# Five seven-product steps instead of four in each column pair of w_down's first half

## The chip, the cores and the metric

The kernel runs on one core of a Trainium2 chip. Its time is the device time of one execution, in microseconds. The engines are called as the profile calls them: PE is TensorE (matmuls; PEld is its weight load), DVE is VectorE, ACT is ScalarE, POOL is GpSimd, SP is the engine whose queue issues most DMAs.

## The reference

One decoder layer on 256 tokens of width 2048, in fp32: a mixing part with two groups of attention heads, and a channel mixer. Only the end of the channel mixer is touched here:

```python
h = rmsnorm(x, pre_ffn_g[l])
u = causal_dwconv(h @ w_up[l], conv_w[l], conv_b[l])
gate, val = jnp.split(u, 2, axis=-1)
y = (jax.nn.gelu(gate, approximate=True) * val) @ w_down[l]
x = x + rmsnorm(y, post_ffn_g[l])
```

`w_up` is 2048 x 11264, `w_down` is 5632 x 2048. Call the product of gelu(gate) and val G: 256 tokens x 5632.

## The kernel before

**Parts.** Every fp32 operand of a matmul is split into a high part (rounded to the matmul's type, a cast on ACT) and a low part (the rest, a subtraction on DVE; `split`, L286 to L288, and `w_split`, L107 to L124). A product is three matmuls: high by high, high by low, low by high (`products`, L973).

**Weights.** `w_load` (L70) fetches 512 KB, 128 x 1024 values, by a DMA on SP's queue into one of five `raw` buffers. `w_parts` (L79) gives one of five pairs of buffers `whi` and `wlo`. ACT casts `whi`, DVE subtracts into `wlo`, PE uses both.

**Stages.** The channel mixer runs in two halves of 22 blocks of 128 columns of G. For each half, first the up projection: eleven steps g of 256 columns, each with a gate and a val projection (`proj_T`), the convolution (`conv`), gelu and the product, after which two blocks of G are split into `G[2g]` and `G[2g+1]` (L950 to L952). A block holds G transposed: 128 channels on the partitions, 256 tokens high and 256 low in the free dimension. Then w_down, in two column pairs, n = 0 and n = 2: columns n and n + 1, 512 wide each, are made together. The first half leaves its sum in `y_sb`, the second half adds to it.

**Fours and sevens.** `four` (L1016) loads two row blocks of w_down for one column group and multiplies them by two token blocks: four products, 12 matmuls. For two column groups that is eight products, 24 matmuls. `seven` (L987) does the same two rows by two column groups by two token blocks in the seven products of Winograd's form, 21 matmuls. It wants sums on both sides. On G's side, with a11, a21 the two token blocks of block 2u and a12, a22 those of block 2u + 1: s1 = a21 + a22, s2 = s1 - a11, s3 = a11 - a21, s4 = a12 - s2. POOL makes them in the up stage (L946 to L949) for the first `most` steps g, and ACT and DVE split them into `sums`. On the weights' side DVE makes four differences in place in the two raw buffers (L998 to L1001), one after another; the blocks are split before (w11; w21 and w22) and after (t1 and t3; t4 and t2). The seven products use a11, a12, a22, s1, s2, s3 and s4; a21 itself is in none of them.

**Order in w_down.** `SEVENS[half][n // 2]` says at which steps i of a column pair a seven stands. A step is: the seven's first three products (a, b, e), a four for column n and a four for n + 1, then the seven's other four products (d, f, c, g). The sevens take the first rows u, the fours the rest, so with four sevens there are seven steps, with five there are six. After the last seven `fold` (L1023) adds the four shared banks into `y_sb`; after the last step `down` (L963, with L965) adds the banks b, g, e and h.

**Who orders what.** PE runs in the order of the program. The instructions of ACT, DVE, POOL and SP are ordered by a planner that goes by its own costs, and each engine then runs its list in that order, waiting for what is not ready.

Of the kernel before, what the change touches and what calls it, by code (L numbers as in the profile page):

```python
# [9 lines left out]
F32R = mybir.dt.float32r  # L10
BF16 = mybir.dt.bfloat16
AF = mybir.ActivationFunctionType
ALU = mybir.AluOpType
# [4 lines left out]
P = 128  # L18
# [6 lines left out]
NEG = -1e30  # L25
FHALF = 22
HOLD = 6
SEVENS = (((0, 1, 3, 4), (0, 1, 3, 4)), ((0, 1, 3, 4), (0, 2)))
LOW = (14, 4, 4, 4)
ROOM = 112  # L30

# [2 lines left out]
def hybrid_layer(ctx: ExitStack, tc: tile.TileContext, x, pre_mix_g, w_in, b_forget, sinks,  # L34
# [3 lines left out]
    pe, act, dve, pool, sp = nc.tensor, nc.scalar, nc.vector, nc.gpsimd, nc.sync  # L38
# [5 lines left out]
    main = ctx.enter_context(tc.tile_pool(name="main", bufs=1))  # L44
# [7 lines left out]
    def bank(tag="acc"):  # L52
        return ps.tile([P, 512], F32, tag=tag, bufs=4, name="bank_" + tag)
# [16 lines left out]
    def w_load(src, a, c, pin=False):  # L70
        raw = wp.tile([P, UNIT], F32, tag="raw", bufs=5, name="raw")
        i = sp.dma_start(raw[:, :a * c].rearrange("p (a c) -> p a c", a=a), src)
        if pin:
            tc.keep_in_program_order(i)
        return raw, a, c
# [53 lines left out]
    def w_rows(w, k0, a, c0, c):  # L129
        return w[k0 * P:(k0 + a) * P, c0:c0 + c].rearrange("(a p) c -> p a c", p=P)  # L130
# [155 lines left out]
    def split(hi, lo, src):  # L286
        act.copy(hi, src)  # L287
        dve.tensor_tensor(lo, src, hi.bitcast(F32), op=ALU.subtract)  # L288
# [531 lines left out]
    with tc.tile_pool(name="ffn", bufs=1) as fp:  # L820
# [46 lines left out]
        def first_gate():  # L867

            banks = [bank(), bank()]

            def v(x, t):
                return x.rearrange("p (h t c) -> p h t c", h=2, t=2)[:, :, t, :]

            def each(kts):
                for kt in kts:
                    for m, b in enumerate(banks):
                        yield kt, b, slice(m * P, (m + 1) * P)

            def gate_high(t, *kts):
                for kt, b, ms in each(range(*kts)):  # L880
                    pe.matmul(v(b, t), gate[kt][0][:, ms], v(hT[:, kt, 0:512], t),  # L881
                              start=(t == 0 and kt == 0), stop=False)

            def gate_low(u):
                for kt, b, ms in each(range(u * 4, u * 4 + 4)):
                    pe.matmul(b[:, 256:512], gate[kt][1][:, ms], hT[:, kt, 0:256],
                              start=False, stop=(kt == KT - 1))

            gate_high(0, KT)
            for high, low in [turn(1, u) for u in range(4)]:  # L890
                high()
                low()
            lows[2]()
            x_squares(1)
            rows = ffn_tables()
            gate_high(1, 1)
            gate_low(0)
            gate_low(1)
            gate_high(1, 1, 4)
            gate_low(2)  # L900
            gate_high(1, 4, KT)
            gate_low(3)
            later(3, rows)
            return banks
# [3 lines left out]
        for half in range(2):  # L908
            G = [fp.tile([P, 512], F32R, tag="G", bufs=FHALF, name=f"G{j}")[:, 0:512]
                 for j in range(FHALF)]  # L910
            most = max(len(at) for at in SEVENS[half])
            if half:
                sums = main.tile([P, 4, 1024], F32R, tag="x", name="sums")
            for g in range(FHALF // 2):
                c0 = (half * (FHALF // 2) + g) * 256
                alt = (g + half) % 2
                if half == 0 and g == 0:
                    bg = first_gate()
                    order.__exit__(None, None, None)
                    bv = [bank(), bank()]  # L920
                    proj_T(w_up, DFF + c0, bv, LONG)
                else:
                    bg = [bank("att"), bank("att")] if alt else [bank(), bank()]
                    proj_T(w_up, c0, bg, LONG)
                gates = []
                for m in range(2):
                    y = conv(bg[m], c0 // P + m, "yg")
                    act.activation(y, y, AF.Gelu_apprx_tanh)
                    gates.append(y)
                if half or g:  # L930
                    bv = [bank("att"), bank("att")] if alt else [bank(), bank()]
                    proj_T(w_up, DFF + c0, bv, LONG)
                ys = []
                for m in range(2):
                    y = conv(bv[m], 44 + c0 // P + m, "yv")
                    dve.tensor_tensor(y, y, gates[m], op=ALU.mult)
                    ys.append(y)
                if g < most:
                    if half == 0 and g == 0:
                        for t in range(2):  # L940
                            sp.dma_start(x_dram[t * P:(t + 1) * P, :], x_sb[:, t, :])
                        sums = main.tile([P, 4, 1024], F32R, tag="x", name="sums")
                    s = fp.tile([P, 512], F32, tag="s", name="s")
                    (a11, a21), (a12, a22) = [(y[:, 0:P], y[:, P:256]) for y in ys]
                    s1, s2, s3, s4 = (s[:, i * P:i * P + P] for i in range(4))
                    pool.tensor_tensor(s1, a21, a22, op=ALU.add)  # L946
                    pool.tensor_tensor(s2, s1, a11, op=ALU.subtract)
                    pool.tensor_tensor(s3, a11, a21, op=ALU.subtract)
                    pool.tensor_tensor(s4, a12, s2, op=ALU.subtract)  # L949
                for m, y in enumerate(ys):  # L950
                    gt = G[g * 2 + m]
                    split(gt[:, 0:256], gt[:, 256:512], y)  # L952
                if g < most:
                    split(sums[:, g, 0:512], sums[:, g, 512:1024], s)
            if half == 1:
                rest = main.tile([P, KT, 512], F32R, tag="hT", name="rest")
                gbf = fp.tile([P, D], F32, tag="gbc", name="gbc_ffn")
# [21 lines left out]
            def parts_of(k, t):  # L979
                return G[k][:, t * P:(t + 1) * P], G[k][:, 256 + t * P:256 + (t + 1) * P]  # L980

            def split_into(dst, src, n):
                hi, lo = (x[:, :n * 512] for x in dst)
                split(hi, lo, src[:, :n * 512])
                return [(hi[:, i:i + 512], lo[:, i:i + 512]) for i in range(0, n * 512, 512)]

            def seven(n, u, last, banks, opened):  # L987

                b, e, g, a, c, d, f = banks
                k = half * FHALF + u * 2  # L990
                top, low = [w_load(w_rows(w_down, k + i, 1, n * 512, 1024), 1, 1024)[0]
                            for i in range(2)]
                b11, b12, b21, b22 = (x[:, i:i + 512] for x in (top, low) for i in (0, 512))
                s1, s2, s3, s4 = [(sums[:, u, i * P:i * P + P],
                                   sums[:, u, 512 + i * P:640 + i * P]) for i in range(4)]
                (w11,) = split_into(w_parts(UNIT, held=False), top, 1)
                w21, w22 = split_into(w_parts(UNIT, held=False), low, 2)
                dve.tensor_tensor(b11, b12, b11, op=ALU.subtract)  # L998
                dve.tensor_tensor(b12, b22, b12, op=ALU.subtract)
                dve.tensor_tensor(b22, b22, b11, op=ALU.subtract)  # L1000
                dve.tensor_tensor(b21, b21, b22, op=ALU.subtract)  # L1001
                products(a, parts_of(u * 2, 0), *w11, opened, last)
                products(b, parts_of(u * 2 + 1, 0), *w21, opened)
                products(e, s4, *w22, opened)

                def others():
                    t1, t3 = split_into(w_parts(UNIT, held=False), top, 2)
                    t4, t2 = split_into(w_parts(UNIT, held=False), low, 2)
                    products(d, s1, *t1, opened, last)
                    products(f, s3, *t3, opened, last)  # L1010
                    products(c, s2, *t2, opened, last)
                    products(g, parts_of(u * 2 + 1, 1), *t4, opened)

                return others
# [30 lines left out]
            for n in (0, 2):  # L1045
                opened = []
                tail = half and n
                at = SEVENS[half][n // 2]
                shared = [bank("att") for _ in range(4 if at else 0)]
                b, e, g = [bank() for _ in range(3)]  # L1050
                h = None if tail else bank()
                for i in range(FHALF // 2 - len(at)):
                    others = None
                    if i in at:
                        u = at.index(i)
# [68 lines left out]
        for t in range(2):  # L1124
            i = sp.dma_start(x_sb[:, t, :], x_dram[t * P:(t + 1) * P, :])
# [5 lines left out]
        v = before_last(0, 3)  # L1131
# [5 lines left out]
        for h in range(2):  # L1137
            if h:
                v = before_last(1, 4)
# [38 lines left out]
```

## Time and profile before

| | us |
|---|---|
| median of 3 runs | 1058.31 (1058.13 to 1058.46) |
| profiled execution | 1058.56 |
| its span, first to last instruction | 1056.8 |
| PE busy | 1046.5 |
| DVE busy | 820.8 |
| ACT busy | 635.5 |
| POOL busy | 259.0 |
| first half's up projections and its w_down, in the span | about 345 to 576 and 576 to 690 |

The profile is one execution, taken by the hardware profiler. Its span leaves out what lies before the first and after the last instruction. Rows of a timeline give start and duration in us, the engine, the line of the kernel, the operation and the tiles it writes and reads; in brackets stands the idle time before it and what ended it. A row of a group gives the count, the busy time and the mean duration in ns. Matmuls overlap: one of 512 columns is shown with 0.39 us, and its neighbour starts sooner than it ends.

### The profile page before, as it was taken

The numbers are of one execution on the slowest core, as the hardware profiler recorded it, in microseconds if no ns is written. First come the engines' busy times: TensorE is split into PE (matmuls) and PEld (weight loads), VectorE is DVE, ScalarE is ACT, GpSimd is POOL, SyncE is SP. The second block draws the span as 40 slices with busy tenths as digits, with TensorE's granted clock in tenths as the row PEclk, the third lists the DMA queues.
The fourth block names the chain that finished last, engine by engine and source line by source line (L and its number), as shares of the span: only waits on it lengthen the run. The fifth ranks groups of instructions, "written<-read, shape, count | busy, mean of one in ns | idle before, by whom it ended". The sixth has DMA issues, their size and how long they took to land.

```text
span 1056.8 us, 16351 instructions
## 1 busy us (share of the span) xinstructions
PE 1046.5 (99%) x5920; PEld 910.4 (86%) x5920; DVE 820.8 (78%) x1324; ACT 635.5 (60%) x1094; POOL 259.0 (25%) x282
## 2 busy tenths in 40 slices
PE   9999999999999999999999999999999999999996
PEld 7889988888889888888888888888888888888786
DVE  5989877886468787777768888867787777788983
ACT  7777757767557656656555555546566565655560
POOL 4253245431122433311112000003432221200301
PEclk9999999999999999999999999999999999999999
DMA  8645666655875766666665566766656665647483
GB/s 291 194 124 180 181 191 202 175 153 161 298 237 186 220 202 196 201 186 199 193 199 149 188 221 204 235 198 192 187 179 210 192 198 186 192 149 233 156 274 126
DMA packets 161965, 207.09 MB, mean 196 GB/s; under 512 B 6844, under 2 KB 131036, under 8 KB 160860
## 3 DMA queue, kind: packets, MB, share of 16 engines
q1 hardware_dynamic: 161564, 205.65, 62.0%
q8 instruction: 46, 0.75, 0.3%
q10 hardware_dynamic: 320, 0.40, 0.1%
q14 instruction: 35, 0.29, 0.1%
HBM read 201.68 MB, written 4.21 MB: 195 GB/s over the span
## 4 chain that ended last, share of the span: by engine, by line
PE 89%; DVE 4%; DMA 2%; issue 2%; ACT 1%; POOL 0%; SPq 0%; DVEq 0%; POOLq 0%; ACTq 0%
PE bank_acc L262 21%; PE bank_att L262 15%; PE bank_acc L284 13%; PE bank_acc L975 12%; PE bank_acc L269 11%; PE bank_att L269 7%; PE bank_att L975 2%; DMA raw<-in_w_down_dram 2%; DVE wlo L121 1%; PE bank_att L450 1%; PE bank_att L485 1%; PE bank_att L494 1%; DVE wlo L288 1%; PE bank_acc L881 1%; PE bank_acc L225 1%
## 5 line engine op out<-in xcount | busy, mean ns | idle before, releaser
L121 DVE TENSOR_TENSOR wlo<-raw,whi 128x1024 fp32r<-128x1024 f32 (+3 forms) x329 | 400.6, 1231 | 121.5 <-ACT whi L118 114.3
L118 ACT CAST whi<-raw 128x1024 fp32r<-128x1024 f32 (+3 forms) x328 | 333.5, 1033 | 174.6 <-issue 84.5
L262 PE MATMUL bank_acc<-hT,whi 128*128 128x512 f32 x1024 | 245.5, 392 | 0.0
L262 PEld LDWEIGHTS bank_acc<-hT,whi 128*128 128x128 f32 x1024 | 188.2, 188 | 37.1
L857 POOL TENSOR_TENSOR u<-u,rowf 128x256 f32<-128x256 f32 x88 | 95.6, 1107 | 440.1 <-DVE u L856 437.2
L262 PE MATMUL bank_att<-hT,whi 128*128 128x512 f32 x704 | 165.7, 390 | 0.0
L975 PE MATMUL bank_acc<-whi,G 128*128 128x512 f32 x492 | 159.5, 389 | 0.0
L262 PEld LDWEIGHTS bank_att<-hT,whi 128*128 128x128 f32 x704 | 130.6, 188 | 26.2
L269 PEld LDWEIGHTS bank_acc<-hT,wlo 128*128 128x128 f32 x1024 | 123.5, 188 | 3.2
L269 PE MATMUL bank_acc<-hT,wlo 128*128 128x256 f32 x1024 | 125.8, 278 | 0.0
L975 PEld LDWEIGHTS bank_acc<-whi,G 128*128 128x128 f32 x492 | 92.4, 188 | 19.0
L975 PE MATMUL bank_acc<-wlo,G 128*128 128x512 f32 x246 | 95.9, 390 | 0.4 <-DVE wlo L121 0.4
L269 PEld LDWEIGHTS bank_att<-hT,wlo 128*128 128x128 f32 x704 | 83.6, 188 | 1.9
L269 PE MATMUL bank_att<-hT,wlo 128*128 128x256 f32 x704 | 84.0, 277 | 0.0
L284 PE MATMUL bank_acc<-whi,oT 128*128 128x512 f32 (+1 forms) x272 | 81.8, 379 | 0.0
L287 ACT CAST whi<-raw 128x1024 fp32r<-128x1024 f32 (+1 forms) x56 | 51.7, 942 | 35.2 <-PE bank_acc L975 15.9
L288 DVE TENSOR_TENSOR wlo<-raw,whi 128x1024 fp32r<-128x1024 f32 (+1 forms) x56 | 62.2, 1133 | 6.5 <-ACT whi L287 6.5
L284 PEld LDWEIGHTS bank_acc<-whi,oT 128*128 128x128 f32 x272 | 50.2, 188 | 9.3
L975 PEld LDWEIGHTS bank_acc<-wlo,G 128*128 128x128 f32 x246 | 46.2, 188 | 10.2 <-DVE wlo L121 0.8
L284 PE MATMUL bank_acc<-wlo,oT 128*128 128x512 f32 (+1 forms) x136 | 51.2, 377 | 0.0
L859 ACT ACTIVATE yg<-u,cw 128x256 f32<-128x256 f32 x44 | 26.5, 602 | 37.2 <-POOL u L857 37.2
L284 PE MATMUL bank_acc<-whi,hT 128*128 128x384 f32 (+1 forms) x192 | 46.9, 323 | 0.0
(250 smaller groups left out, 1317.7 us busy)
## 6 DMA issues: line engine op xcount, KB each, us to landing
raw<-in_w_up_dram SPq DMA_DIRECT2D x176, 512.0 KB, 4.5
raw<-in_w_down_dram SPq DMA_DIRECT2D x88, 512.0 KB, 4.9
raw<-in_w_in_dram SPq DMA_DIRECT2D x51, 512.0 KB, 5.0
raw<-in_w_out_dram SPq DMA_DIRECT2D x32, 512.0 KB, 4.6
raw<-in_w_in_dram SPq DMA_DIRECT2D x16, 384.0 KB, 3.3
cb<-c_dram SPq DMA_DIRECT2D x8, 256.0 KB, 4.5
x_sb<-in_x_dram SPq DMA_DIRECT2D x2, 1024.0 KB, 6.0
x_dram<-x_sb SPq DMA_DIRECT2D x2, 1024.0 KB, 5.8
```

What stands on the lines that cost most here:

```text
L118: i1 = act.copy(hi[:, cs], raw[:, cs])
L121: i2 = dve.tensor_tensor(lo[:, cs], raw[:, cs], hi[:, cs].bitcast(F32), op=ALU.subtract)
L225: pe.matmul(b, hi[:, a, m * P:(m + 1) * P], hT[:, kt, 0:512], start=(kt == 0), stop=(kt == KT - 1))
L262: pe.matmul(b, hi[:, a, m * P:(m + 1) * P], hT[:, kt, 0:512], start=(kt == 0), stop=(last == (0, kt)))
L269: pe.matmul(b[:, 256:512], lo[:, a, m * P:(m + 1) * P], hT[:, u * 4 + a, 0:256], start=False, stop=(last == (1, u * 4 + a)))
L284: pe.matmul(b, a, r[:, cols], start=(first and i == 0), stop=(last and i == 2))
L287: act.copy(hi, src)
L288: dve.tensor_tensor(lo, src, hi.bitcast(F32), op=ALU.subtract)
L450: pe.matmul(sb[e][:, cs], a[r, t * P:(t + 1) * P], b[r, 0:nk], start=(n == 0), stop=(n == 2))
L857: pool.tensor_tensor(u[:, 2:258], u[:, 2:258], rowf, op=ALU.mult)
L859: act.activation(y, u[:, 2:258], AF.Identity, bias=cw[:, 3, ch:ch + 1], scale=cw[:, 2, ch:ch + 1])
L975: pe.matmul(b, x, r, start=b not in opened and not i, stop=closes and i == 2)
```

## The change

In the first half, each column pair gets five sevens, at steps 0 to 4, instead of four at steps 0, 1, 3 and 4. So the fifth pair of row blocks moves from fours to a seven, and a column pair has six steps instead of seven. The second half keeps its sevens.

Five sums of 4 KB a partition would not fit into the 16 KB of `sums`. In the first half s1 is therefore written over a21 in the product's own tile, before G is split, and takes a21's place in the block of G; `sums` keeps s2, s3 and s4, 384 wide, high and low 3 KB. In both halves POOL's instruction for s3 comes first, since it reads a21, and s1 stands last in `s` and `sums`.

```diff
-SEVENS = (((0, 1, 3, 4), (0, 1, 3, 4)), ((0, 1, 3, 4), (0, 2)))
+SEVENS = (((0, 1, 2, 3, 4), (0, 1, 2, 3, 4)), ((0, 1, 3, 4), (0, 2)))
...
-                sums = main.tile([P, 4, 1024], F32R, tag="x", name="sums")
+                sums = main.tile([P, 4096], F32R, tag="x", name="sums")
...
                     (a11, a21), (a12, a22) = [(y[:, 0:P], y[:, P:256]) for y in ys]
-                    s1, s2, s3, s4 = (s[:, i * P:i * P + P] for i in range(4))
+                    s2, s3, s4, s1 = (s[:, i * P:i * P + P] for i in range(4))
+                    if not half:
+                        s1 = a21
+                    pool.tensor_tensor(s3, a11, a21, op=ALU.subtract)
                     pool.tensor_tensor(s1, a21, a22, op=ALU.add)
                     pool.tensor_tensor(s2, s1, a11, op=ALU.subtract)
-                    pool.tensor_tensor(s3, a11, a21, op=ALU.subtract)
                     pool.tensor_tensor(s4, a12, s2, op=ALU.subtract)
                 for m, y in enumerate(ys):
                     gt = G[g * 2 + m]
                     split(gt[:, 0:256], gt[:, 256:512], y)
                 if g < most:
-                    split(sums[:, g, 0:512], sums[:, g, 512:1024], s)
+                    w = 384 + 128 * half
+                    split(*(sums[:, i * w:i * w + w] for i in (2 * g, 2 * g + 1)), s[:, :w])
...
-                s1, s2, s3, s4 = [(sums[:, u, i * P:i * P + P],
-                                   sums[:, u, 512 + i * P:640 + i * P]) for i in range(4)]
+                w = 384 + 128 * half
+                s2, s3, s4, s1 = [[sums[:, v * w + i * P:v * w + i * P + P]
+                                   for v in (2 * u, 2 * u + 1)] for i in range(4)]
+                if not half:
+                    s1 = parts_of(u * 2, 1)
```

More of the change, by code (lines that the diff above doesn't have):

```diff
@@ L941, in hybrid_layer @@
                             sp.dma_start(x_dram[t * P:(t + 1) * P, :], x_sb[:, t, :])
-                        sums = main.tile([P, 4, 1024], F32R, tag="x", name="sums")
+                        sums = main.tile([P, 4096], F32R, tag="x", name="sums")
                     s = fp.tile([P, 512], F32, tag="s", name="s")
                     (a11, a21), (a12, a22) = [(y[:, 0:P], y[:, P:256]) for y in ys]
-                    s1, s2, s3, s4 = (s[:, i * P:i * P + P] for i in range(4))
+                    s2, s3, s4, s1 = (s[:, i * P:i * P + P] for i in range(4))
+                    if not half:
+                        s1 = a21
+                    pool.tensor_tensor(s3, a11, a21, op=ALU.subtract)
                     pool.tensor_tensor(s1, a21, a22, op=ALU.add)
                     pool.tensor_tensor(s2, s1, a11, op=ALU.subtract)
-                    pool.tensor_tensor(s3, a11, a21, op=ALU.subtract)
                     pool.tensor_tensor(s4, a12, s2, op=ALU.subtract)
```

## The prediction

> **What bounds the kernel now.** I read the page's busy times first, then what TensorE (PE) waited for over the whole span.
>
> ```profile
> PE 1046.5 (99%) x5920; PEld 910.4 (86%) x5920; DVE 820.8 (78%) x1324; ACT 635.5 (60%) x1094; POOL 259.0 (25%) x282
> PE bank_acc L173 <- DVE junk L168: 1.3, 1, 1.3
> PE bank_att L494 <- DVE pl L288: 0.5, 1, 0.5
> PE bank_acc L975 <- DVE wlo L121: 0.4, 1, 0.4
> ```
>
> PE is busy for 99% of the span, and its named waits come to 2.2 us. So a matmul less is time less, as long as the others keep PE fed. The stretches view of the first half's w_down stage (columns: us of the stretch; busy us and count of PE, PEld, DVE, ACT, POOL; clock; DMA share; GB/s) and the chain of waits at the end of its first column pair (start, us, what) say the same of the place that changes:
>
> ```profile
> 575.50:692.00 116.50, 116.50 (x516) 96.47 (x515) 100.37 (x116) 63.17 (x69) 2.22 (x2) 1.00 0.65 210
> ```
> ```profile
> 612.67 6.80 PE bank_acc L975 x30
> 619.48 2.04 PE bank_att L975 x9
> 621.51 11.56 PE bank_acc L975 x51
> 633.08 0.68 PE bank_att L975 x3
> ```
>
> PE has no gap here, its clock is 1.00, and a 512-column matmul takes 6.80/30 = 0.2267 us. DVE is busy for 100.37 of 116.50 us: it is the engine with the least room. ACT and the DMAs have much more.
>
> **Matmuls removed.** Two fours (rows u of columns n and n+1) are 24 matmuls; a seven in their place is 21. One more seven in each of two column pairs saves 6 x 0.2267 = **1.36 us**. The matmul count should fall from 5920 to 5914. The 44 loads of 512 KB in this stage stay 44: a seven's two rows replace one load of each four.
>
> **DVE and ACT work added.** Groups of this stage (count | busy us, mean ns | idle before):
>
> ```profile
> L121 DVE TENSOR_TENSOR wlo<-raw,whi 128x1024 fp32r<-128x1024 f32 x32 | 38.9, 1222 | 11.5 <-ACT whi L118 11.2
> L288 DVE TENSOR_TENSOR wlo<-raw,whi 128x1024 fp32r<-128x1024 f32 x23 | 27.6, 1222 | 3.6 <-ACT whi L287 3.6
> L998 DVE TENSOR_TENSOR raw<-raw 128x512 f32<-128x512 f32 x7 | 4.8, 690 | 0.2
> L288 DVE TENSOR_TENSOR wlo<-raw,whi 128x512 fp32r<-128x512 f32 x7 | 4.8, 685 | 1.3 <-ACT whi L287 1.3
> L118 ACT CAST whi<-raw 128x1024 fp32r<-128x1024 f32 x31 | 32.6, 1054 | 30.9 <-PE bank_acc L975 21.6 <-DMA raw<-in_w_down_dram 5.5 <-PE bank_att L975 2.1
> L287 ACT CAST whi<-raw 128x512 fp32r<-128x512 f32 x7 | 4.3, 620 | 2.6 <-DMA raw<-in_w_down_dram 2.5
> ```
>
> A seven costs DVE three 1024-wide low parts, one 512-wide and four differences: 3 x 1.22 + 0.69 + 4 x 0.69 = 7.1 us. The two fours cost 2.45. So DVE gets 4.6 us more in each pair, and ACT (3 x 1.05 + 0.62) - 2 x 1.05 = 1.7 us more. ACT's hides in the 30.9 us that it waits before L118, mostly for PE to free a weight buffer. DVE's is the question: in a loop step with a seven it does 7.1 + 2.45 = 9.5 us of work under 45 matmuls, 10.2 us. Neighbours on DVE overlap by some 0.08 us (two L121 end 2.35 us after the first starts, below, not 2.44), which makes it about 9.1, so DVE gains some 1 us on PE in a step, if it never idles. Five such steps now follow one another, where the third was a pause of fours with 2.3 us of DVE work under 5.4 us of matmuls.
>
> By the Trainium skill, "VectorE: DVE Perf Modes", section "The perf-mode tier table", an fp32 tensor_tensor from SBUF runs at 1x, 2293 ns for 2048 elements. By that figure the step's 7,680 elements are an estimated 8.6 us, a margin of 1.6 us instead of 1; the rows say 9.1 to 9.5, and I use the rows.
>
> **Where that shows first: the third step of pair one.** DVE's and PE's timelines (start, us, line, out<-in [idle before <- releaser]):
>
> ```profile
> 591.27 1.05 ACT L287 CAST whi<-raw 128x1024 fp32r<-128x1024 f32 x1 [2.42 <-DVE raw L1001]
> 592.35 1.23 DVE L288 TENSOR_TENSOR wlo<-raw,whi 128x1024 fp32r<-128x1024 f32 x1 [1.19 <-ACT whi L287]
> 604.38 2.96 DVE L288 TENSOR_TENSOR wlo<-raw,whi 128x1024 fp32r<-128x1024 f32 x3
> 611.30 2.35 DVE L121 TENSOR_TENSOR wlo<-raw,whi 128x1024 fp32r<-128x1024 f32 x2
> ```
> ```profile
> 595.06 0.39 PE L975 MATMUL bank_att<-wlo,sums 128*128 128x512 f32 x1
> 598.46 0.39 PE L975 MATMUL bank_acc<-wlo,G 128*128 128x512 f32 x1
> ```
>
> The last unit of the second seven is ready on DVE at 593.58 and its low part is used at 595.06, a lead of only 1.5 us. Today DVE then has two fours to do. With a seven there, PE reaches the first four's low part after 3 + 6 + 2 matmuls more, at 598.46. DVE needs for w11, four differences, w21/w22 and that four what it took at the fifth step: from 606.74 (the second of the three at 604.38 ends, 0.60 before the third) to 612.52 (the first of the two at 611.30 ends), 5.78 us. 593.58 + 5.78 = 599.36: **0.9 us late**. If the planner puts the four ahead of the last two differences, as it did in some steps, it is 1.4 us sooner and nothing is late. Bounds 0 and 0.9; I take 0.3, nearer to none, because in the other steps of this pair DVE got each four done in time.
>
> The loads are next in question: SP issues one when DVE is through with a buffer, and a seven keeps its two until its last low parts. SP's waits, the loads of this stage (median us to landing) and ACT's longest wait for one:
>
> ```profile
> SPq L72 <- DVE wlo L121: 78.9, 36, 6.1
> raw<-in_w_down_dram SPq DMA_DIRECT2D x38, 512.0 KB, 4.9
> 599.70 1.05 ACT L118 CAST whi<-raw 128x1024 fp32r<-128x1024 f32 x1 [2.80 <-DMA raw<-in_w_down_dram]
> ```
>
> Buffers come free in the same order as now, so the load that lands before 599.70 becomes the top row of the fourth step's seven, wanted by PE only at 606.6. Cost nothing; were it a four of the third step, up to the 2.8 us.
>
> **And the border to pair two.** After the last seven there are now two fours, 24 matmuls or 5.44 us, less until pair two, while the four reads of the fold (L1029 to L1032) and the four of L965 stay (group first, then the timelines):
>
> ```profile
> L965 DVE TENSOR_TENSOR y_sb<-bank_acc,y_sb 128x512 f32<-128x512 f32 x8 | 5.1, 682 | 0.0
> ```
> ```profile
> 613.57 2.35 DVE L288 TENSOR_TENSOR wlo<-raw,whi 128x1024 fp32r<-128x1024 f32 x2
> 617.88 1.23 DVE L121 TENSOR_TENSOR wlo<-raw,whi 128x1024 fp32r<-128x1024 f32 x1 [0.82 <-ACT whi L118]
> 620.70 1.23 DVE L121 TENSOR_TENSOR wlo<-raw,whi 128x1024 fp32r<-128x1024 f32 x1 [1.59 <-ACT whi L118]
> 622.67 1.23 DVE L121 TENSOR_TENSOR wlo<-raw,whi 128x1024 fp32r<-128x1024 f32 x1 [0.15 <-ACT whi L118]
> 633.47 1.28 DVE L965 TENSOR_TENSOR y_sb<-bank_acc,y_sb 128x512 f32<-128x512 f32 x2
> ```
> ```profile
> 620.90 0.39 PE L975 MATMUL bank_att<-wlo,sums 128*128 128x512 f32 x1
> 634.27 0.39 PE L975 MATMUL bank_acc<-whi,sums 128*128 128x512 f32 x1
> ```
>
> From 615.92 to the third read of L965 (633.47 + 0.68 = 634.15) are 18.2 us, 2.56 of them idle; without two L121 (2.3) the work is 13.4 us. PE used the unit of 615.92 at 620.90 and needs that bank at 634.27; 5.44 us sooner, that is 615.92 + 12.9. So the bank e is freed **0.5 us late**, if the order stays; with that read ahead of the L121 before it, not at all. Bounds 0 and 0.8 (0.8 if the lead at the last seven is 0.3 us shorter); I take 0.2. Pair two's end has no such border: there up-projection units follow, whose DVE work is light. Sum of the stalls: **0.5 us, bounds 0 and 1.7**.
>
> **The up stage.** A fifth group of four sums (POOL), one more cast and one more low part, each 384 instead of 512 wide, and G's split of the first y now waits for POOL's s1. The groups of tile s, and what the second group does to ACT, DVE and PE:
>
> ```profile
> L948 POOL TENSOR_TENSOR s<-yv x8: 2319/2322/2382, 363.4 to 783.4; 128x128 f32<-128x128 f32 x8
> L946 POOL TENSOR_TENSOR s<-yv x8: 455/458/461, 365.7 to 785.6; 128x128 f32<-128x128 f32 x8
> ```
> ```profile
> 388.53 0.62 ACT L287 CAST sums<-s 128x512 fp32r<-128x512 f32 x1 [3.14 <-POOL s L949]
> 389.18 0.69 DVE L288 TENSOR_TENSOR sums<-s,sums 128x512 fp32r<-128x512 f32 x1 [2.50 <-ACT sums L287]
> 389.79 2.35 DVE L121 TENSOR_TENSOR wlo<-raw,whi 128x1024 fp32r<-128x1024 f32 x2
> 393.45 3.82 PE L269 MATMUL bank_acc<-hT,wlo 128*128 128x256 f32 x32
> ```
>
> POOL already runs L948 first, so moving it changes nothing; G's split waits 2.32 + 0.46 us, inside the 3.14 us that ACT waits anyway. Queued behind it on ACT and DVE are the next weights' parts: the last one ends at 392.14, and PE reads it at 393.45 + 3 x 0.91 = 396.2, so 4 us of cover are left. Five narrower splits (at most 0.62 + 0.69 each) against four wide ones are one more at the most, 1.3 us spread over five steps. Cost: nothing; were the cover gone, 3.1 us.
>
> L948 is five times L946 at one size. The Trainium skill, "SBUF — State Buffer", section "SBUF: two separate sides", has VectorE and GpSimd take turns on one port pair for whole instructions; the trace agrees. By that rule all four sums could wait for a 1.2 us DVE instruction each: an estimated 3 us more, still inside the 4 us.
>
> **Sum.** The profiled execution took 1058.56 us, 1.76 around its span of 1056.8. 1058.56 - 1.36 + 0.5 = 1057.7; the median shown, 1058.31, is 0.25 below that execution, so **1057.45 us**.
>
> **Rivals.** *Nothing is late* (the planner orders around both places): 1058.31 - 1.36 = 1056.95. For: PE had no gap in the stage. Against: the lead of 1.5 us.
> *Both places late in full*: 1058.31 - 1.36 + 1.7 = 1058.65. For: the order that the steps from the fourth on show.
> *DVE becomes the bound*, the other side. Place: the round trip L1001, ACT's cast, DVE's low part, in which DVE idled 1.19 us at 592.35. If it comes back in each seven, a step is 9.1 + 1.2 = 10.3 us on DVE against 10.2, the lead of 1.5 us never recovers, and the stalls add: 0.9 + 0.8 at the two places, 0.9 again in pair two, and 0.1 in each of 10 steps, 3.6 in all: 1060.55. It decides once DVE idles over 1 us in a step. Against: pair two idles less.
> *The second half gets better too*, if the planner's new order spares it this gap of PE:
>
> ```profile
> 996.12 0.50 PE L975 MATMUL bank_acc<-wlo,G 128*128 128x512 f32 x1 [0.42 <-DVE wlo L121]
> ```
>
> Then 1056.95 - 0.42 = 1056.5, lower only if it saves more there. Against: nothing in that half is edited but the places of the sums.
>
> **How the numbers follow.** Forecast 0.47, nothing late 0.26, both late 0.14, DVE the bound 0.09, the second half better 0.04. A measurement here tells 0.2%, 2.1 us, from no change, so 1056.2 and 1060.4 are the marks. Only DVE as the bound passes the upper one, and most of the last rival's chance stays above the lower: faster 0.03, same 0.88, slower 0.09. The range goes from 1056.3, a little under the last rival, to 1059.7, both places late and 0.1 lost in each of ten steps.
>
> **What would show it.** 5914 matmuls; the stage at 575.5 shorter by 0.9 us, down to 115.1 long if nothing is late; PE's gaps, if any, before L975 on DVE's wlo in the third step of pair one and on L965's bank at the start of pair two; DVE over 94% busy in the stage; no new PE wait before 575. A PE gap in the up stage, or in three steps or more, would prove me wrong.

## The result, and the profile after

| | before | changed |
|---|---|---|
| median of 22 executions, us | 1058.26 | 1059.2 |
| lowest to highest, us | 1057.73 to 1058.83 | 1058.57 to 1062.43 |
| ratio, 95% interval | | 1.0014, 1.0007 to 1.002 |
| profiled execution, us | 1058.56 | 1062.43 |
| its span, us | 1056.8 | 1060.7 |

The changed kernel is slower by 0.14%, some 0.9 us. That is inside the forecast range and below the 0.2% that the prediction took as the mark. But the forecast was 0.86 us faster than the median shown, so 1.75 us went somewhere. The changed kernel's executions also spread further than those of before, 3.9 us against 1.1. The profiled execution is the slowest of the 22. A second profiled execution of the same kernel took 1059.42, near the median; I call it "again".

The busy times of the changed kernel, and its PE waits that are new or longer:

```profile
PE 1047.8 (99%) x5914; PEld 910.9 (86%) x5914; DVE 830.9 (78%) x1337; ACT 639.1 (60%) x1099; POOL 261.1 (25%) x286
PE bank_acc L978 <- DVE wlo L121: 1.7, 1, 1.7
PE bank_acc L978 <- DVE y_sb L968: 1.2, 2, 0.8
```

The six matmuls are gone, 5920 to 5914, and DVE has 10 us more, about the 9.2 that the prediction worked out. There are three new waits of PE, all in one place. L968 and L978 are the lines L965 and L975 of before, L1004 to L1007 its L998 to L1001, L1035 to L1038 its L1029 to L1032. The stretches view (columns as in the prediction) of the changed kernel and of "again" shows the place:

```profile
575.50:692.00 116.50, 113.52 (x492) 92.88 (x491) 102.93 (x121) 64.12 (x73) 2.22 (x2) 0.99 0.61 199
633.00:644.00 11.00, 8.02 (x26) 5.52 (x25) 10.16 (x14) 3.68 (x5) 0.00 (x0) 0.84 0.29 89
```
```profile
633.00:644.00 11.00, 9.01 (x39) 6.81 (x38) 10.66 (x13) 3.37 (x4) 0.00 (x0) 1.00 0.42 151
```

Over the stage DVE is busy for 102.93 of 116.50 us, 88%, so it isn't the bound of the stage as a whole; in the 11 us after 633, where pair two begins, it is busy for 10.16 and, in "again", for 10.66. PE is busy there for 8.02 in the first profile, and the clock, 1.00 in "again", is 0.84. PE's timeline there in the first profile (start, duration, line, tiles, matmuls, [wait <- releaser]):

```profile
633.02 0.39 PE L978 MATMUL bank_att<-whi,G 128*128 128x512 f32 x1
633.88 0.47 PE L978 MATMUL bank_acc<-whi,G 128*128 128x512 f32 x1 [0.47 <-DVE y_sb L968]
...
634.41 0.40 PE L978 MATMUL bank_acc<-whi,G 128*128 128x512 f32 x1
635.58 0.50 PE L978 MATMUL bank_acc<-whi,sums 128*128 128x512 f32 x1 [0.77 <-DVE y_sb L968]
...
636.38 0.40 PE L978 MATMUL bank_acc<-whi,G 128*128 128x512 f32 x1
638.51 0.72 PE L978 MATMUL bank_acc<-wlo,G 128*128 128x512 f32 x1 [1.74 <-DVE wlo L121]
...
642.26 0.40 PE L978 MATMUL bank_acc<-wlo,G 128*128 128x512 f32 x1
```

I count a pause as the time from one matmul's start to the next, less 0.2267. There are three: before product b (633.88 - 633.02 - 0.23 = 0.63), before product e (635.58 - 634.41 - 0.23 = 0.94), and before the low part of the first four (638.51 - 636.38 - 0.23 = 1.90), 3.47 us together. After the last one the matmuls themselves are slow: from 638.51 to 642.26 nine intervals take 3.75 us, 0.42 each, 1.71 more than at 0.2267. The stretches view gives a granted clock of 0.50 for 638.60 to 642.00, and 1.00 for 633 to 638.60. With the 1.36 us saved, 3.47 + 1.71 - 1.36 = 3.8; the two profiled executions differ by 1062.43 - 1058.56 = 3.87. That these meet so closely is partly chance. Set matmul by matmul against the profile before, the changed one is 0.33 us behind when the stage begins, 4.40 when it ends, and 3.90 at the end of the kernel, since PE's wait at 996 in the profile before is gone. The stage itself makes 4.07 us: the 3.8, and some 0.2 in the first intervals after the first two pauses, which the count above leaves out.

In "again" the pauses are 0.44, 1.89 and two of 0.11, together 2.55 us, and no matmul is slow. Its PE timeline around the two long ones:

```profile
633.59 0.39 PE L978 MATMUL bank_acc<-whi,G 128*128 128x512 f32 x1
634.25 0.50 PE L978 MATMUL bank_acc<-whi,sums 128*128 128x512 f32 x1 [0.28 <-DVE y_sb L968]
...
635.07 0.40 PE L978 MATMUL bank_acc<-whi,G 128*128 128x512 f32 x1
637.18 0.50 PE L978 MATMUL bank_acc<-wlo,G 128*128 128x512 f32 x1 [1.72 <-DVE wlo L121]
```

**What DVE does meanwhile.** Its timeline before and after the change, from the fold on, first before:

```profile
625.61 0.68 DVE L1032 TENSOR_TENSOR y_sb<-bank_att,y_sb 128x512 f32<-128x512 f32 x1
...
629.40 1.22 DVE L121 TENSOR_TENSOR wlo<-raw,whi 128x1024 fp32r<-128x1024 f32 x1
630.54 1.28 DVE L965 TENSOR_TENSOR y_sb<-bank_acc,y_sb 128x512 f32<-128x512 f32 x2
631.74 0.68 DVE L1001 TENSOR_TENSOR raw<-raw 128x512 f32<-128x512 f32 x1
```
```profile
625.92 1.23 DVE L121 TENSOR_TENSOR wlo<-raw,whi 128x1024 fp32r<-128x1024 f32 x1 [2.89 <-ACT whi L118]
...
629.51 0.69 DVE L1005 TENSOR_TENSOR raw<-raw 128x512 f32<-128x512 f32 x1 [1.04 <-DMA raw<-in_w_down_dram]
630.12 0.68 DVE L1035 TENSOR_TENSOR y_sb<-bank_att,y_sb 128x512 f32<-128x512 f32 x1
...
634.25 0.68 DVE L1006 TENSOR_TENSOR raw<-raw 128x512 f32<-128x512 f32 x1
634.85 1.88 DVE L968 TENSOR_TENSOR y_sb<-bank_acc,y_sb 128x512 f32<-128x512 f32 x3
636.64 0.68 DVE L1007 TENSOR_TENSOR raw<-raw 128x512 f32<-128x512 f32 x1
637.24 2.35 DVE L121 TENSOR_TENSOR wlo<-raw,whi 128x1024 fp32r<-128x1024 f32 x2
```

Two things differ. Before, the fold ended ahead of the differences, and the first four's low part (L121 at 629.40) stood ahead of all reads of L965 and of the last difference. Now the planner has put the first difference of the lower row (L1005) ahead of the fold, and the first four's low part behind the whole fold, all four reads of L968 and both last differences. And in the first profile L1005 waits for the load of that lower row; the fold stands behind it, though its banks are full from about 626 on (fold_first, below). The loads issued from 610 to 632 in the changed kernel (count, KB each, median us to landing; the profile tells the landing of three of them):

```profile
raw<-in_w_down_dram SPq DMA_DIRECT2D x9, 512.0 KB, 8.4
```

The median is 8.4 us here, against 4.9 in the whole stage of before. But in this window it was 6.1 before, too, and it is 6.7 in "again". What differs in both profiles is the issue. The load of the lower row, the 24th of the stage, was issued at 617.08 before and landed after 6.9 us. In "again" it was issued at 620.67, once DVE was through with a low part of the fifth seven and so with its buffer, and landed after 6.5; in the first profile it was issued at 620.79 and landed after 8.6. ACT shows the wait, 2.83 us for the lower row in the first profile:

```profile
629.52 1.05 ACT L287 CAST whi<-raw 128x1024 fp32r<-128x1024 f32 x1 [2.83 <-DMA raw<-in_w_down_dram]
```

In "again" the lower row is there in time for DVE, and it is the top row that holds ACT and then DVE up:

```profile
626.07 0.62 ACT L287 CAST whi<-raw 128x512 fp32r<-128x512 f32 x1 [1.83 <-DMA raw<-in_w_down_dram]
626.72 0.69 DVE L288 TENSOR_TENSOR wlo<-raw,whi 128x512 fp32r<-128x512 f32 x1 [1.23 <-ACT whi L287]
```

So there are three candidates for the loss at the border. **L**: pair two's first rows land late and hold DVE up. **W**: DVE has too much to do, in the wrong order, between the last seven and the first four. **The clock**: some executions lose more through slow matmuls after the pauses. The rivals were that the new layout of the sums costs the time, and that five sevens in a row do.

### The profile page after: what moved, and what is told of

The parts are those of the page before. It is cut to its first block, busy times and chain, and to the rows that moved or that the text cites. A ratio compares the mean times of both kernels' runs of the same rounds, so it can differ in the third digit from the quotient of the medians.

```text
span 1060.7 us, 16372 instructions
## 1 busy us (share of the span) xinstructions
PE 1047.8 (99%) x5914; PEld 910.9 (86%) x5914; DVE 830.9 (78%) x1337; ACT 639.1 (60%) x1099; POOL 261.1 (25%) x286
## 4 chain that ended last, share of the span: by engine, by line
PE 87%; DVE 5%; issue 2%; DMA 2%; ACT 1%; POOL 1%; SPq 0%; DVEq 0%; POOLq 0%; ACTq 0%
PE bank_acc L262 20%; PE bank_att L262 15%; PE bank_acc L284 13%; PE bank_acc L978 12%; PE bank_acc L269 10%; PE bank_att L269 8%; PE bank_att L978 3%; DVE wlo L121 2%; DMA raw<-in_w_down_dram 1%; DVE wlo L288 1%; PE bank_att L450 1%; PE bank_att L485 1%; PE bank_att L494 1%; PE bank_acc L881 1%; DMA x_in<-in_x_dram 1%
## 5 line engine op out<-in xcount | busy, mean ns | idle before, releaser
L121 DVE TENSOR_TENSOR wlo<-raw,whi 128x1024 fp32r<-128x1024 f32 (+3 forms) x325 | 395.7, 1232 | 116.9 <-ACT whi L118 111.0
L118 ACT CAST whi<-raw 128x1024 fp32r<-128x1024 f32 (+3 forms) x324 | 329.3, 1032 | 163.3 <-issue 83.0
L978 PE MATMUL bank_acc<-whi,G 128*128 128x512 f32 x468 | 154.3, 392 | 0.5 <-DVE y_sb L968 0.5
L978 PEld LDWEIGHTS bank_acc<-whi,G 128*128 128x128 f32 x468 | 88.7, 190 | 19.1 <-ACT whi L118 0.9
L978 PE MATMUL bank_acc<-wlo,G 128*128 128x512 f32 x234 | 92.0, 393 | 1.7 <-DVE wlo L121 1.7
L287 ACT CAST whi<-raw 128x512 fp32r<-128x512 f32 (+1 forms) x64 | 58.7, 942 | 45.5 <-PE bank_acc L978 15.2
L288 DVE TENSOR_TENSOR wlo<-raw,whi 128x512 fp32r<-128x512 f32 (+1 forms) x64 | 70.1, 1121 | 6.5 <-ACT whi L287 6.3
L978 PEld LDWEIGHTS bank_acc<-wlo,G 128*128 128x128 f32 x234 | 44.3, 189 | 11.6 <-DVE wlo L121 2.5
```

What stands on the lines that cost most here:

```text
L118: i1 = act.copy(hi[:, cs], raw[:, cs])
L121: i2 = dve.tensor_tensor(lo[:, cs], raw[:, cs], hi[:, cs].bitcast(F32), op=ALU.subtract)
L978: pe.matmul(b, x, r, start=b not in opened and not i, stop=closes and i == 2)
```

## The experiments

Each was compared with the kernel before, on the same chip. Medians and ranges are of 11 executions. "Pauses" is the sum of PE's pauses at the border in its one profiled execution. "Sum" is 1058.11 (the median of before in the first comparison; 1058.08 and 1058.16 in the two later ones), less 0.227 for each matmul saved, plus the pauses.

| kernel | median (range), us | ratio [95%] | pauses | sum |
|---|---|---|---|---|
| again | 1059.42 (one execution) | | 2.55 | 1059.30 |
| layout_only | 1057.95 (1057.82 to 1058.64) | 0.9998 [0.9989, 1.0007] | 0 | 1058.11 |
| five_pair1 | 1059.91 (1058.61 to 1063.29) | 1.0020 [1.0011, 1.0029] | 2.60 | 1060.03 |
| five_pair2 | 1057.47 (1056.98 to 1058.4) | 0.9992 [0.9983, 1.0001] | 0 | 1057.43 |
| spare_raw | 1058.14 (1057.56 to 1061.74) | 1.0003 [0.9994, 1.0012] | 1.20 | 1057.92 |
| fold_first | 1057.54 (1057.43 to 1058.42) | 0.9994 [0.9985, 1.0003] | 0.74 | 1057.46 |
| keep_warm | 1059.56 (1058.84 to 1060.16) | 1.0013 [1.0004, 1.0022] | 2.27 filled + 0.58 | 1059.57 |
| shift_pair2 | 1057.79 (1057.05 to 1057.95) | 0.9995 [0.9986, 1.0004] | 0.87 | 1057.59 |
| defer | 1057.53 (1056.64 to 1058.37) | 0.9993 [0.9984, 1.0002] | 0.82 | 1057.62 |
| spare_defer | 1056.85 (1056.52 to 1057.83) | 0.9987 [0.9978, 0.9996] | 0 | 1056.80 |
| fold_spare | 1057.71 (1057.27 to 1058.27) | 0.9996 [0.9987, 1.0005] | 0.74 | 1057.54 |

The sums stand within 0.25 us of the medians. By the times alone only five_pair1, keep_warm and spare_defer can be told from before, since the other intervals hold 1; what is said of the others rests on the pauses, in one trace each. Of keep_warm's 0.58 some 0.2 lie later in pair two, at 668, and of shift_pair2's 0.87 the part of 0.33 lies at the start of the next stage. Pauses of that size elsewhere aren't in the sums: the wait of 0.42 at 996 in the profile of before, which none of the other twelve profiles shows at that size, and waits of 0.2 to 0.8 for `x_in` in some of them.

### Which half of the change costs: again, layout_only, five_pair1, five_pair2

**again** has no edit. **layout_only** keeps the sums in 3 KB and s1 in G, but leaves four sevens, and so four groups of sums in the first half:

```diff
-SEVENS = (((0, 1, 2, 3, 4), (0, 1, 2, 3, 4)), ((0, 1, 3, 4), (0, 2)))
+SEVENS = (((0, 1, 3, 4), (0, 1, 3, 4)), ((0, 1, 3, 4), (0, 2)))
```

**five_pair1** and **five_pair2** have the fifth seven in one pair alone. The other pair uses the fifth block in a four and so needs its a21; for that block s1 stays in `sums`, behind the others:

```diff
-SEVENS = (((0, 1, 2, 3, 4), (0, 1, 2, 3, 4)), ((0, 1, 3, 4), (0, 2)))
+SEVENS = (((0, 1, 2, 3, 4), (0, 1, 3, 4)), ((0, 1, 3, 4), (0, 2)))    # five_pair1
+SEVENS = (((0, 1, 3, 4), (0, 1, 2, 3, 4)), ((0, 1, 3, 4), (0, 2)))    # five_pair2
...
-                    if not half:
+                    if not half and g < 4:
                         s1 = a21
...
+                    if not half and g == 4:
+                        split(sums[:, 3072:3584], sums[:, 3584:4096], s)
```

> The changed kernel once more, for a second profile. Its profiled execution was 1062.43 us, its median 1059.2: the times spread from 1058.6 to 1062.4, those of the kernel before only from 1057.7 to 1058.8. Theory (border and clock): PE stands still at the start of pair two each time, some 3.5 us in the first profile, and only where the pause is long enough does the granted clock fall to a half for about 3.4 us, worth 1.6 us more. Then an execution near 1058.8 shows gaps at the same three places (before the products b, e and the first four) of 1.5 to 2.5 us in all and no matmul with a start-to-start of 427 ns. Rival (the gap itself comes and goes): an execution near 1058.8 shows no gap at one of the three places.

> Only the layout: sums 384 wide, s1 in the place of a21, s3 first on POOL; four sevens a pair as before. Theory (border): the layout costs nothing, 1058.3 as before, within 0.3, and PE has no gap in the first half. Rival (the layout pays: splits of G waiting for POOL, other places of the sums): 1058.8 or more, with a PE gap in the up stage or a longer DVE instruction.

> Five sevens in pair one only, four in pair two; the s1 of the fifth lies in sums, so that a21 stays in G for pair two's fours. Theory (border): the fours between pair one's last seven and pair two are two as in the changed kernel, so the stall at the start of pair two is there: 0.68 saved, 1.5 to 5 lost, 1059.2 to 1062.5. Rival (the stall comes from five sevens in a row, wherever): about half of the changed kernel's loss, 1058.8, and gaps inside the pair.

> Five sevens in pair two only, four in pair one. Theory (border): four fours lie between pair one's last seven and pair two, as in the kernel before, and after pair two comes the up projection, which wants little of DVE: no gap of PE, 0.68 saved, 1057.6. Rival (five sevens in a row are too much for DVE): a gap in pair two and 1058.3 or more.

"again" took 1059.42, 1.31 above before: even without a slow matmul the pauses are there, 2.55 us in all. But there are two places and not three: before product b there is none, so a part of the loss does come and go, as the rival had it. The layout alone is worth nothing measurable, 1057.95 against 1058.11, so that rival falls. five_pair1 shows the loss, and more of it, since it saves half as much; here are its waits of PE for DVE at the border, and after them the three longest waits of PE in five_pair2, none of which lies in this stage:

```profile
PE bank_acc L981 <- DVE wlo L121: 1.7, 1, 1.7
PE bank_acc L981 <- DVE y_sb L971: 0.3, 1, 0.3
```
```profile
PE bank_acc L173 <- DVE junk L168: 1.3, 1, 1.3
PE bank_att L494 <- DVE pl L288: 0.4, 1, 0.4
PE bank_att L309 <- DMA x_in<-in_x_dram: 0.3, 1, 0.3
```

five_pair2 has five sevens in a row too and no pause at any of them; its median is 0.64 us lower where three matmuls are 0.68. So it isn't the five in a row, and it isn't pair two's sevens: the loss is at the border behind a pair one that ends with two fours instead of four.

### Loads, order and clock: spare_raw, fold_first, keep_warm, shift_pair2

**spare_raw** tests L. The two rows of pair two's first seven go into a buffer that is free at that time, so their loads wait for no `raw` buffer; DVE's order at the border stays.

```diff
-                top, low = [w_load(w_rows(w_down, k + i, 1, n * 512, 1024), 1, 1024)[0]
-                            for i in range(2)]
+                if not half and n and not u:
+                    spare = fp.tile([P, D], F32, tag="gbc", name="spare")
+                    top, low = spare[:, 0:1024], spare[:, 1024:2048]
+                    for i, x in enumerate((top, low)):
+                        sp.dma_start(x, w_rows(w_down, k + i, 1, n * 512, 1024)
+                                     .rearrange("p a c -> p (a c)"))
+                else:
+...
```

**fold_first** tests the order alone: pair two's first seven may be given out only after the last instruction of the fold.

```diff
-                        others = seven(n, u, u == len(at) - 1, (b, e, g, *shared), opened)
+                        with tc.issue_after(folded[0].ins) if folded and n and not i and not half \
+                                else ExitStack():
+                            others = seven(n, u, u == len(at) - 1, (b, e, g, *shared), opened)
```

**keep_warm** tests the clock: ten matmuls into a bank that is opened afresh later fill the pauses. Their products are thrown away.

```diff
+                idle = (0, 2, 8) if half == 0 and n == 2 and u == 0 else (0, 0, 0)
+                def spin(k):
+                    for _ in range(k):
+                        pe.matmul(c, parts_of(u * 2, 0)[0], w11[0], start=True, stop=True)
                 products(a, parts_of(u * 2, 0), *w11, opened, last)
+                spin(idle[0])
                 products(b, parts_of(u * 2 + 1, 0), *w21, opened)
+                spin(idle[1])
                 products(e, s4, *w22, opened)
+                spin(idle[2])
```

**shift_pair2** lets pair two begin with a step of fours and its five sevens come one step later (the bank g is then closed by the last seven):

```diff
-SEVENS = (((0, 1, 2, 3, 4), (0, 1, 2, 3, 4)), ((0, 1, 3, 4), (0, 2)))
+SEVENS = (((0, 1, 2, 3, 4), (1, 2, 3, 4, 5)), ((0, 1, 3, 4), (0, 2)))
```

> The changed kernel, but the two rows of w_down for pair two's first seven lie in a tile that is unused in this half (the place of gbc_ffn) and are loaded long before; every order at the border stays as it is in the changed kernel. In the second profile of that kernel (1059.42 us) DVE idled 1.36 and 1.23 us before pair two, when ACT waited 2.32 and 1.83 us for loads, and PE lost 0.4 and 1.9 us; in the first (1062.43) the lower row landed 2.2 us later still. Theory L (late loads): with the two rows there, DVE does w11 and the first two differences ahead of the fold and has 2.6 us more: the stall falls to under 0.5 us, 1058.1 - 1.36 + 0.3 = 1057.0, and the spread up to 1062 goes. Theory W (work and order): the fold's four reads, the four of L968 and two differences stand before the first four on DVE, whatever is loaded: 1.9 us lost there, 1058.6 to 1059.

> The changed kernel, but on DVE, ACT and SP's side nothing is taken away: only pair two's first seven has its DVE instructions queued behind the fold's last one. The planner then sets on DVE fold, two reads of L968, w11, w21/w22, two reads of L968, one difference, the first four's low part. Theory W (work and order): what PE waits for longest, the first four's low part, comes after one difference instead of four and three more instructions: stall under 0.7 us, 1056.8 to 1057.4. Theory L (late loads): the load of the lower row decides, and lands no sooner: the stall stays 2 us or more, 1059.

> The changed kernel with ten matmuls more at the start of pair two, two before product e and eight before the first four, 10 x 0.227 = 2.3 us, into a bank that is opened afresh afterwards; the instruction order of DVE there is as in the changed kernel. They stand where PE waited 0.4 and 1.9 us, so they should cost about nothing. Theory (the spread is the clock): PE no longer pauses for over 1 us, the granted clock stays, no run of matmuls with 427 ns, and the times above 1060.4 (8 of 22) go: all within 1058.5 to 1059.9. Rival (the spread is the loads): the times still reach 1061 or more, with the clock at full speed.

> Five sevens in both pairs, those of pair two at its steps 1 to 5 instead of 0 to 4, so that four fours lie between the last seven of pair one and the first of pair two, as in the kernel before; the fold of pair two then meets the up projection. Theory (border): no gap at the start of pair two; at its end the next projection's second bank waits for the fold's first read, at most 0.5 us: 1058.1 - 1.36 + 0.3 = 1057.0. Rival (ten sevens are too much for DVE): a gap somewhere in pair two, 1058.1 or more.

**spare_raw**: neither theory has it all. With the rows there in time the pauses fall from 2.55 to 1.20 us, so L is worth 1.35 with DVE's order as it is; the rest stays. No row of pair two holds DVE up any more (a wait of 1.30 for pair one's last four stays): the fold starts at 627.22 instead of 628.79 in "again", and the first four's low part comes at 634.34 instead of 635.91:

```profile
627.22 0.69 DVE L1042 TENSOR_TENSOR y_sb<-bank_att,y_sb 128x512 f32<-128x512 f32 x1
634.34 2.35 DVE L121 TENSOR_TENSOR wlo<-raw,whi 128x1024 fp32r<-128x1024 f32 x2
```
```profile
628.79 0.68 DVE L1035 TENSOR_TENSOR y_sb<-bank_att,y_sb 128x512 f32<-128x512 f32 x1
...
635.91 2.35 DVE L121 TENSOR_TENSOR wlo<-raw,whi 128x1024 fp32r<-128x1024 f32 x2
```

One of its 11 executions took 1061.74, at a mean clock of 0.996. So the spread did not go with the late rows, as theory L had expected.

**fold_first** takes pauses of 1.81 away with the order alone; the top row's cast starts at 625.63, hardly sooner than in "again", 626.07. What is left, 0.74, and the median, 1057.54, are a little over what theory W had expected. The fold starts when PE has written its banks, at 626.23, and the four's low part comes at 633.77:

```profile
626.23 0.69 DVE L1035 TENSOR_TENSOR y_sb<-bank_att,y_sb 128x512 f32<-128x512 f32 x1 [1.68 <-PE bank_att L978]
633.77 1.22 DVE L121 TENSOR_TENSOR wlo<-raw,whi 128x1024 fp32r<-128x1024 f32 x1
```

So L and W are not two terms to be added: the late row costs because the fold stands behind the instruction that waits for it.

**keep_warm** asks about the upper times. Of the changed kernel's 22 executions, 7 took over 1060.4 us (the expectation has 8; it is 7), and all of these had a mean clock of 0.996; the other 15 had 0.997 to 0.999. With the pauses filled, none of 11 is over 1060.16, at a median 0.36 higher than the changed kernel's; two are over the 1059.9 that was expected. That fits the pauses bringing the slow matmuls about. It isn't a proof: in five_pair1 an execution of 1061.9 us had 0.997 and one of 1063.29 had 0.994, and I have the trace of one such case alone. The mean clock is a coarse sign, too. A stretch of 3.4 us at 0.50 lowers it by 0.0016 of a span of 1060.7. The clock behind the last matmul counts as well: in the profile before it is 0.50 from 1053.7 to the end, and the last matmul starts at 1048.6. So 0.997 doesn't rule such a stretch out. How much of the spread is the clock and how much the loads stays open.

**shift_pair2** is a bit slower than expected, 1057.79. A pause of 0.54 stays at the bank g, which the first four now writes in its second product, and 0.33 comes new at the next stage's start, together 0.87. The other 2.0 us at the border are gone: the two fours at the start of pair two need a low part each and no difference.

### A version that beats both: defer, spare_defer, fold_spare

**defer** moves the two last differences of pair two's first seven (L1006, L1007), which only t2 and t4 need, from before the first four to behind it. **spare_defer** is defer with spare_raw, **fold_spare** is fold_first with spare_raw.

```diff
+                wait = not half and n and not u
-                dve.tensor_tensor(b22, b22, b11, op=ALU.subtract)
-                dve.tensor_tensor(b21, b21, b22, op=ALU.subtract)
+                def last_two():
+                    dve.tensor_tensor(b22, b22, b11, op=ALU.subtract)
+                    dve.tensor_tensor(b21, b21, b22, op=ALU.subtract)
+                if not wait:
+                    last_two()
...
                 def others():
+                    if wait:
+                        last_two()
```

> The changed kernel, but in pair two's first seven the third and fourth difference (L1006, L1007, 1.3 us on DVE) come after the two fours instead of before; DVE then does fold, one read of L968, the first four's low part, three reads of L968. Theory (two shares: late loads 1.35 us, order on DVE 1.2 us, as the runs with the spare tile and with the fold first show): only the share of the order goes; the first four's low part is 1.3 + 1.8 us sooner, bank e's read 0.6 us later, so PE loses about 1.0 us in place of 2.5: 1058.1 - 1.36 + 1.0 = 1057.8. Rival (all of it is late loads, the order matters only through them): the stall stays over 2 us, 1058.9.

> Both: the spare tile for the two rows and the two differences after the fours. Theory (two shares that add up to the whole): no gap at the start of pair two, the full 1.36 us saved, 1056.7 to 1057.0, and no time above 1058. Rival (something else of ten sevens costs too): 1057.4 or more.

> The spare tile and the fold first on DVE. DVE's list from the fold to the first four's low part is then as in the run with the fold first, and it starts only when PE has finished the last seven's third product. Theory (DVE's work between that product and the first four is the limit: 4 reads of the fold, 4 of L968, w11, w21/w22, one difference and the four, 8.8 us against 8.1): the loads no longer matter, the same gap of 0.6 us as with the fold first, 1057.5. Rival (what is left there comes from loads): no gap, 1056.9.

defer did better than expected, 1057.53: the four's pause is gone, and a pause of 0.82 stays at bank e (0.55 in "again"), whose read on DVE still stands behind the late row and now behind the four's low part as well:

```profile
PE bank_acc L978 <- DVE y_sb L968: 0.5, 1, 0.5
```

spare_defer has no pause at the border at all. PE's and DVE's timelines where the changed kernel had its last one:

```profile
634.08 0.39 PE L978 MATMUL bank_acc<-whi,G 128*128 128x512 f32 x1
634.30 0.39 PE L978 MATMUL bank_acc<-wlo,G 128*128 128x512 f32 x1
```
```profile
631.12 1.21 DVE L121 TENSOR_TENSOR wlo<-raw,whi 128x1024 fp32r<-128x1024 f32 x1
632.25 1.87 DVE L968 TENSOR_TENSOR y_sb<-bank_acc,y_sb 128x512 f32<-128x512 f32 x3
```

The four's low part runs at 631.12, ahead of the last three reads of L968, and is done at 632.33, two us before PE wants it. Moving two instructions of 0.68 us was enough for the planner to put the four's low part ahead of these reads again, as in the kernel before; the first two differences still stand ahead of the fold. It takes 1056.85, 0.9987 of before, 1.31 us less where six matmuls are 1.36, and its executions lie within 1.3 us. Measured in other comparisons, so against the changed kernel only by the medians, it is 2.35 us faster.

fold_spare gains nothing over fold_first: the same 0.74 us is left.

```profile
PE bank_acc L978 <- DVE wlo L121: 0.5, 1, 0.5
```

Once the fold goes first, the row's arrival no longer matters, and what is left is DVE's work between the fold and the first four.

## Why the prediction was wrong

**Right.** The matmuls saved are 6, worth 1.36 us: five_pair2's median is 0.64 lower for three, spare_defer's 1.31 for six, and in their traces the stage has no pause. The up stage costs nothing: layout_only has the new places of the sums, without the fifth group, and stays at before; the changed kernel has both, and set against the profile before it is 0.35 us behind when the up stage begins and 0.33 when it ends. DVE's 10 us more in the stage were foreseen, and so were the two places to look at: bank e of the border is one of the three pauses.

**Too high: the third step of pair one, 0.3.** Nothing was late there, which is the lower bound. The planner put the step's four between two differences, as the prediction named it for that case; DVE is through at 597.39, and PE uses it at 598.79.

```profile
596.17 1.22 DVE L121 TENSOR_TENSOR wlo<-raw,whi 128x1024 fp32r<-128x1024 f32 x1
597.30 0.69 DVE L1005 TENSOR_TENSOR raw<-raw 128x512 f32<-128x512 f32 x1
```

**Wrong: the border to pair two, 0.2 with bounds 0 and 0.8.** It took 2.55 us in "again" and 3.47 in the first profile, where slow matmuls came on top with 1.71. This step failed, in three parts.

- *The order on DVE.* The prediction followed the bank e alone, by the old order of DVE "if the order stays". The order didn't stay, and it was the first four, whose low part had 629.40 in the old list, that came out 1.7 to 1.9 us late. The term had to be taken at this later use, and not at bank e: ahead of it DVE has four reads of the fold, four of L968, five low parts (the four's own with them) and four differences to do, and of the four fours that gave it time before only two, 5.44 us, are left.
- *The loads.* "Buffers come free in the same order as now", and so "Cost nothing", was looked at for the fourth step's row only, and by the order, not the time. Five sevens in pair one free them later. The load of pair two's lower row was issued at 617.08 before, at 616.62 in layout_only and at 617.11 in five_pair2, which have four there; with five it was issued at 620.26 in five_pair1, 620.67 in "again" and 620.79 in the first profile. The first profile's 8.6 us to land, against 6.5 to 6.9 in "again" and before, came on top. With DVE's order as it was, the late rows were worth 1.35 us (spare_raw); with the fold first they are worth nothing (fold_spare).
- *The clock.* No rival had it that a pause of PE costs more than itself.

With 2.5 in the place of 0.2 and 0 in the place of 0.3, the prediction's own sum is 1057.45 - 0.5 + 2.5 = 1059.45, against a median of 1059.2.

**The rivals.** *Nothing is late*, 1056.95, is what spare_defer makes of it, 1056.85. *Both places late in full* had the time nearest to the result, 1058.65, though for a wrong reason: one place was late, by thrice its bound. *DVE becomes the bound* is refuted in its mechanism: its round trip is there behind the second seven, as before, and behind the third, with the same 1.19 us,

```profile
602.66 2.96 DVE L288 TENSOR_TENSOR wlo<-raw,whi 128x1024 fp32r<-128x1024 f32 x3 [1.19 <-ACT whi L287]
```

but no step of the stage beside the border has a PE pause, and DVE is at 88%. *The second half gets better*: the wait of 0.42 at 996 is in no later profile at that size. In layout_only, which changes little but the places of the sums, this is worth 0.49 us against the profile before. But before was traced once, so whether the wait was there each time stays open, and the median of layout_only, 0.16 us under before, is within the interval.

**What it named as proof against itself**, a PE gap in the up stage or in three steps or more, didn't come. Its other sign failed: the stage was to be 0.9 us shorter, and it is 4.1 us longer in the first profile and 1.2 in "again". The gaps were at the border where it looked, but the largest was at a tile that it didn't name, the first four's low part, and their size was wrong.

## What to carry to other kernels

Price a border by its last user: sum up all that an in-order engine has to do between the last heavy step of one stage and the first needs of the next, set it against the cover that is left, and don't trust the engine's mean share. When cover is taken away, ask when the buffers come free, not only in which order, which instruction of the list waits for a load, and what urgent work stands behind it; moving two short instructions, or loading two rows into a buffer of their own, was worth 1 to 1.7 us here, about what the change itself saves. And keep a spread of executions in sight: where pauses appear, some executions may pay more than the pause.

## What the runs showed of the hardware

**The clock after short pauses.** In the first profile pauses of 0.63, 0.94 and 1.90 us, with three or four matmuls between, were followed by nine intervals of 0.42 us on average where 0.227 is usual; the granted clock was 0.50 from 638.60 to 642.00, which makes the 0.84 over 11 us. In "again" pauses of 0.44 and 1.89 were followed by none, at 1.00. Why the one and not the other, these runs don't show. The Trainium skill, "TensorE: Matmul & The Clock Gate", section "What's actually happening", has the clock halved after an idle window of about 3.4 us. The trace agrees in the size, 0.42 against 0.227, but no single pause here is that long; the three together are 3.47.

**A load's time varies, and its issue can matter more.** The same 512 KB take 4.9 us to land in the median over the stage of before. In the window from 610 to 632, with nine loads issued each time, the median is 6.1 before, 6.7 in "again" and 8.4 in the first profile; the cause of the 8.4 isn't shown. In "again" the lower row landed late although its load took no longer than before, 6.5 us against 6.9: it was issued 3.6 us later.
